# Split pieces of v kept in DRAM by the backward scan for the forward scan, and the head norm of o moved to ScalarE, in a hybrid Fourier and gated-linear-attention encoder

## The chip, the cores and the metric

One core of a Trainium2 chip runs the whole program. The metric is the device time of one execution in microseconds (us), lower is better. PE is TensorE, PEld its weight loads, DVE is VectorE, ACT is ScalarE, POOL is GpSimd, and SP is SyncE, whose in-order queue issues nearly all of the DMAs here.

## The reference

One encoder layer on x (1 x 2048 x 1024), all in float32, and a final RMSNorm. Cut to what matters here:

```
h    = rmsnorm(x) * (1 + scale) + shift
proj = h @ w_in                     # u, z, q, k, v, r and two gate logits
y_f  = fourier_mix(u) * silu(z)
o    = gla(q, k, v, forward) + flip(gla(flip q, flip k, flip v, backward, strict))
o    = o * rsqrt(mean(o*o, per head) + EPS)        # 4 heads of 256 values
y_g  = o * norm_g * silu(r)
x    = x + gate * (concat(y_f, y_g) @ w_out)
out  = rmsnorm(x)
```

`gla` is a chunked linear attention: per chunk, masked scores times v, plus the decayed query times a running state, and the state is updated with the decayed key (transposed) times v.

## The kernel before

The sequence is cut into 16 pieces of 128 rows, numbered `sc`, and into 8 blocks `blk` of two pieces. The 4 heads are worked in two pairs, `hp` = 0 and 1. Every product that needs float32 accuracy is made of three passes over split operands: `hi` is the operand rounded to the matmul type by an ACT copy, `lo` is the rest, by a DVE subtraction (helper `split`, L47 to L49), and the passes are hi.hi, hi.lo and lo.hi. So v has the pieces `vh` and `vl` of 128 x 512, made in `load_v` (L577) from `v`, which comes from the DRAM tensor `v_d` (`vd_`).

In order of the program: projections of the second half of the rows; the backward scan over blocks 7 to 4 (`scan_back`, L589) mixed with further projections (`block_col`, L272, whose weights `raw` are loaded, split into tiles `B` and stored to `bcol_d` for the other half); the Fourier branch and the projections of the first half; the backward scan over blocks 3 to 0, mixed first with projections and then with the splitting of the output weights (`wot` to `wo_hi`, `wo_lo`, L1044 to L1049) and six pieces of the Fourier part of the output projection (`out_fourier`); then the forward scan over the 16 pieces. In the forward scan piece `sc` runs through `core_fwd` (L750: loads, scores `sc`, `sf`, its split `sh` and `sl`, the products `on`, and `update`, which transposes the key to `ktr`, splits it to `kth` and `ktl`, makes `upd` on PE and `state` on DVE), then `tail_fwd` (L795: squares `jk` on ACT, `rstd` on POOL, the head norm of `o`, transposes `otr` on PE, product with `sr` on DVE), then `split_y` (`ghi`, `glo`), and one piece later `out_fwd` (L862: 96 or 192 matmuls `po`, L842, on `ghi`, `glo` and, for pieces not done ahead, `fhi`, `flo`; then `gated_add`, L847 and L848, and the last norm). `prework` (L484) prepares queries and keys of a block with `Exp` and `Ln` on ACT and many steps on DVE.

The order on each engine isn't the order of the code: the build lists all instructions by a scheduler of its own, with its own idea of how long each takes, and hands out buffers as it goes. So an edit at one place can move instructions far from it. On the chip each engine, and the SP queue, then works its list strictly in order; an instruction that waits holds up all that stand behind it.

Buffers that matter: `v`, `vh`, `vl`, `o` and (in the full form) `S` have two each; `v`'s two are also used for `y`, the Fourier part of `load_yf`. A buffer of `vh` is free when the last `upd` matmul that reads it is done.

Of the kernel before, what the change touches and what calls it, by code (L numbers as in the profile page):

```python
# [12 lines left out]
F32 = mybir.dt.float32  # L13
F32R = mybir.dt.float32r
BF16 = mybir.dt.bfloat16
U8 = mybir.dt.uint8
AF = mybir.ActivationFunctionType
ALU = mybir.AluOpType
# [3 lines left out]
P = 128  # L22
# [13 lines left out]
def hybrid_kernel(ctx, tc, i, out):  # L36
    nc = tc.nc
    V, S, G, T = nc.vector, nc.scalar, nc.gpsimd, nc.tensor
    KO = tc.keep_in_program_order

    def load(dst, src):
        nc.sync.dma_start(dst, src)

    def store(dst, src):
        nc.sync.dma_start(dst, src)

    def split(hi, lo, src, eng=None):  # L47
        S.activation(hi, src, AF.Copy)  # L48
        (eng or V).tensor_tensor(lo, src, hi.bitcast(F32), ALU.subtract)  # L49
# [9 lines left out]
    dram = ctx.enter_context(tc.tile_pool(name="dram", bufs=1, space=DRAM))  # L59
# [11 lines left out]
    od_ = dram.tile([16, 2, P, 512], F32, name="ob_d")  # L71
    sst_ = dram.tile([2, P, 512], F32, name="st_d")
    xd_ = dram.tile([16, P, D], F32, name="xf_d")
    us_ = dram.tile([P, NG, 16, 2, P], F32, name="us_d")
    bc_ = dram.tile([12, 7, P, 1024], F32, name="bcol_d")
    bt_ = dram.tile([4, 14, P, BW], F32, name="btok_d")
# [468 lines left out]
    def scores(d, pre, s):  # L545
        qi, ki, Q, K, _ = pre
        ps = pg.tile([P, 2, 192], F32, tag="sc", name="sc")
        kof, qof = (0, 128) if d == 0 else (64, 0)
        for h in range(2):
            g = 2 * h + s  # L550
            c0 = h * 256 + s * P
            T.matmul(ps[:, h, 0:128], ki[:, c0:c0 + P], qi[:, c0:c0 + P], start=True, stop=True)  # L552
            T.matmul(ps[:, h, 128:192], K[:, g, kof:kof + P], Q[:, g, qof:qof + 64], start=True, stop=True)  # L553
        return ps

    def update(d, pre, s, v, state, first):
        K, dec = pre[3], pre[4]
        kof = 64 if d == 0 else 0
        tp = pg.tile([P, 512], F32, tag="tr", name="ktr")
        kth = gp_.tile([P, 2, P], F32R, tag="kth", name="kth", bufs=1)  # L560
        ktl = gp_.tile([P, 2, P], F32R, tag="ktl", name="ktl", bufs=1)
        for h in range(2):
            T.transpose(tp[:, h * P:(h + 1) * P], K[:, 2 * h + s, kof:kof + P], ident[:])
        split(kth[:], ktl[:], tp[:, 0:256].rearrange("p (h t) -> p h t", h=2))
        up_ = pg.tile([P, 2, 256], F32, tag="big", name="upd", bufs=n_v)
        for h in range(2):
            hs = slice(h * 256, (h + 1) * 256)
            mm3(up_[:, h, :], [(kth[:, h, :], ktl[:, h, :], v[0][:, hs], v[1][:, hs])])
        for h in range(2):
            if first:  # L570
                V.tensor_copy(state[:, h, :], up_[:, h, :])
            else:
                g = 2 * h + s
                V.scalar_tensor_tensor(state[:, h, :], state[:, h, :], dec[:, g:g + 1], up_[:, h, :],  # L574
                                       ALU.mult, ALU.add)

    def load_v(sc, hp):  # L577
        v = gp_.tile([P, 512], F32, tag="v", name="v", bufs=n_v)
        load(v[:], vd_[sc, :, hp * 512:(hp + 1) * 512])
        vh = gp_.tile([P, 512], F32R, tag="vh", name="vh")  # L580
        vl = gp_.tile([P, 512], F32R, tag="vl", name="vl")
        S.activation(vh[:], v[:], AF.Copy)  # L582
        V.tensor_tensor(vl[:], v[:], vh[:].bitcast(F32), ALU.subtract)
        return vh, vl

    def states():
        return [gp_.tile([P, 2, 256], F32, tag=f"state{h}", name=f"state{h}", bufs=1) for h in range(2)]

    def scan_back(blk, hp, gt, st_b):  # L589
        pre = prework(1, blk, hp, gt)  # L590
        for s in (1, 0):
            sc = 2 * blk + s
            v = load_v(sc, hp)
            ps = scores(1, pre, s)
            sb = gp_.tile([P, 2, P], F32, tag="S", name="sb", bufs=n_v)
            S.activation(sb[:], ps[:, :, 0:128], AF.Copy)
            V.tensor_copy(sb[64:128, :, 0:64], ps[64:128, :, 128:192])
            store(sd_[sc, hp], sb[:].rearrange("p h t -> p (h t)"))
            if sc != 15:
                ob = pg.tile([P, 2, 256], F32, tag="big", name="ob", bufs=n_v)  # L600
                for h in range(2):
                    T.matmul(ob[:, h, :], pre[2][:, 2 * h + s, 64:192], st_b[hp][:, h, :],
                             start=True, stop=True)
                obs = gp_.tile([P, 512], F32, tag="o", name="obs")
                S.activation(obs[:], ob[:].rearrange("p h t -> p (h t)"), AF.Copy)
                store(od_[sc, hp], obs[:])
            if sc != 0:
                update(1, pre, s, v, st_b[hp], sc == 15)
# [141 lines left out]
    def core_fwd(sc, pre, st_f):  # L750
        s = sc % 2
        os_ = []
        for hp in range(2):
            v = load_v(sc, hp)
            sb = gp_.tile([P, 2, P], F32, tag="S", name="sf", bufs=n_v)
            load(sb[:].rearrange("p h t -> p (h t)"), sd_[sc, hp])
            ps = scores(0, pre[hp], s)
            V.copy_predicated(sb[:], mask[:].rearrange("p (h t) -> p h t", h=2), ps[:, :, 0:128])
            V.tensor_copy(sb[0:64, :, 64:128], ps[0:64, :, 128:192])
            sh = gp_.tile([P, 2, P], F32R, tag="sh", name="sh", bufs=1)  # L760
            sl = gp_.tile([P, 2, P], F32R, tag="sl", name="sl", bufs=1)
            split(sh[:], sl[:], sb[:])
            on = pg.tile([P, 2, 256], F32, tag="big", name="on", bufs=2)
            for h in range(2):
                hs = slice(h * 256, (h + 1) * 256)
                for k, (a_, b_) in enumerate(((sh, v[0]), (sh, v[1]), (sl, v[0]))):
                    T.matmul(on[:, h, :], a_[:, h, :], b_[:, hs], start=(k == 0), stop=(sc == 0 and k == 2))  # L767
                if sc != 0:
                    T.matmul(on[:, h, :], pre[hp][2][:, 2 * h + s, 0:128], st_f[hp][:, h, :],  # L769
                             start=False, stop=True)  # L770
            o = gp_.tile([P, 512], F32, tag="o", name="o")
            onf = on[:].rearrange("p h t -> p (h t)")
            if sc != 15:
                load(o[:], od_[sc, hp])
                V.tensor_tensor(o[:], o[:], onf, ALU.add)  # L775
                update(0, pre[hp], s, v, st_f[hp], sc == 0)
            else:
                V.tensor_copy(o[:], onf)
            os_.append(o)
        return os_  # L780

    def rstd(ss, n, width):
        r = op.tile([P, 4], F32, tag="rstd", name="rstd", bufs=4)
        G.tensor_scalar(r[:, 0:n], ss, 1.0 / width, EPS, ALU.mult, ALU.add)  # L784
        G.tensor_tensor(r[:, 0:n], r[:, 0:n], mhalf[:, 0:n], ALU.pow)  # L785
        return r
# [8 lines left out]
    def tail_fwd(sc, os_, sr):  # L795
        for hp in range(2):
            o = os_[hp]
            ss = op.tile([P, 2], F32, tag="ss", name="ss", bufs=4)
            for h in range(2):
                jk = op.tile([P, 512], BF16, tag="jk", name="jk", bufs=1)  # L800
                S.activation(jk[:, 0:256], o[:, h * 256:(h + 1) * 256], AF.Square, accum_out=ss[:, h:h + 1])  # L801
            r = rstd(ss[:], 2, 256)
            for h in range(2):
                V.tensor_scalar(o[:, h * 256:(h + 1) * 256], o[:, h * 256:(h + 1) * 256], r[:, h:h + 1], None,  # L804
                                ALU.mult)
            tp = pg.tile([P, 4, P], F32, tag="tr", name="otr")
            for c in range(4):
                T.transpose(tp[:, c, :], o[:, c * P:(c + 1) * P], ident[:])  # L808
            y = sr[:, 4 * hp:4 * hp + 4, :]
            V.tensor_tensor(y, tp[:], y, ALU.mult)  # L810
        return sr
# [280 lines left out]
    gt = gates(0)  # L1092
    pre = [prework(0, 0, hp, gt) for hp in range(2)]
    os_ = core_fwd(0, pre, st_f)
    for sc in fo:
        out_fourier(sc)
# [86 lines left out]
```

## Time and profile before

| | |
|---|---|
| median of 3 runs | 1669.92 us (1668.64 to 1671.33) |
| the profiled execution: its own time | 1670.82 us |
| the profiled execution: its span | 1669.0 us |
| granted TensorE clock, mean | 0.978 |
| PE busy | 1570.0 us, 94% |
| DVE busy | 1176.3 us, 70% |
| ACT busy | 695.7 us, 42% |
| DMA moved | 399.90 MB, mean 240 GB/s |

The span is the time from the first to the last instruction; what lies around it is 1.8 us. A share of busy time is a mean over stages, so the stages are read one by one: the backward scan with projections from about 205 to 440 us, its second part from about 1030 to 1200 us, the forward scan from about 1200 to 1640 us, and an end of 29 us. An engine that stands idle costs nothing unless PE waits for it, so the waits of PE come first.

### The profile page before, as it was taken

The page shows a single profiled execution, that of the slowest core. Times are in us where ns is not written, and L with a number is a line of the kernel's source. Part 1 is how long each engine was busy: PE and PEld are TensorE (multiplying, and loading weights), DVE is VectorE, ACT ScalarE, POOL GpSimd, SP SyncE. Part 2 cuts the span into 40 slices and gives each one's busy share as a digit, 9 for nine tenths or more (in the row PEclk, how much of TensorE's full clock was granted, in tenths as well). Part 3 has the DMA queues.
Part 4 walks back from the last instruction along what each step waited for, and adds up shares of the span by engine and source line. Part 5 has one row for each costly group of instructions (what it writes and reads, how often), then busy time and mean ns, then how long its engine had stood idle before and what let it go on. Part 6 is the DMA issues. An engine that isn't in the chain of part 4 may idle for free. (4 is left out here: it accounts for less than half of the span.)

```text
span 1669.0 us, 25145 instructions
## 1 busy us (share of the span) xinstructions
PE 1570.0 (94%) x9012; PEld 1352.1 (81%) x9012; DVE 1176.3 (70%) x2424; ACT 695.7 (42%) x1295; POOL 60.4 (4%) x118
## 2 busy tenths in 40 slices
PE   7899999999988999989989999979989999999997
PEld 5599878888888979889988888767868778878876
DVE  3976687898588265868775646678876776777673
ACT  4724244544244011323232317676644554555442
POOL 0000000000000000000000000000011111101110
PEclk9999999999999999999999999979999999999999
DMA  9599788888885799797888598777653434434422
GB/s 347 201 358 391 264 310 324 321 300 289 306 325 214 255 338 326 235 315 255 272 267 269 172 325 286 236 239 246 226 160 128 123 130 133 147 96 145 143 89 76
DMA packets 220044, 399.90 MB, mean 240 GB/s; under 512 B 19472, under 2 KB 121744, under 8 KB 216336
## 3 DMA queue, kind: packets, MB, share of 16 engines
q1 hardware_dynamic: 219776, 398.04, 69.3%
q8 instruction: 71, 1.16, 0.3%
q14 instruction: 53, 0.43, 0.1%
q10 hardware_dynamic: 144, 0.26, 0.0%
HBM read 237.60 MB, written 160.63 MB: 239 GB/s over the span
## 5 line engine op out<-in xcount | busy, mean ns | idle before, releaser
L272 PE MATMUL pj<-A_hi,B 128*128 128x512 f32 x1344 | 435.9, 399 | 6.7 <-ACT B L48 2.8
L315 PE MATMUL pj<-B,A_hi 128*128 128x264 f32 (+1 forms) x1792 | 336.7, 288 | 21.1 <-ACT p L322 5.8
L315 PEld LDWEIGHTS pj<-B,A_hi 128*128 128x128 f32 x1792 | 282.9, 192 | 26.9 <-ACT p L322 6.5
L272 PEld LDWEIGHTS pj<-A_hi,B 128*128 128x128 f32 x1344 | 251.8, 189 | 64.8 <-ACT B L48 3.7
L272 PE MATMUL pj<-A_lo,B 128*128 128x512 f32 x672 | 268.2, 399 | 0.0
L315 PE MATMUL pj<-B,A_lo 128*128 128x264 f32 (+1 forms) x896 | 255.3, 287 | 2.3 <-DVE A_lo L49 2.3
L315 PEld LDWEIGHTS pj<-B,A_lo 128*128 128x128 f32 x896 | 172.4, 193 | 2.5 <-DVE A_lo L49 2.5
L272 PEld LDWEIGHTS pj<-A_lo,B 128*128 128x128 f32 x672 | 126.8, 189 | 27.4 <-issue 0.2
L842 PE MATMUL po<-wo_hi,fhi 128*128 128x512 f32 x256 | 108.5, 424 | 11.0 <-ACT fhi L48 7.3
L842 PE MATMUL po<-wo_hi,ghi 128*128 128x512 f32 x256 | 103.9, 406 | 2.0 <-ACT ghi L48 2.0
L842 PE MATMUL po<-wo_lo,fhi 128*128 128x512 f32 x256 | 105.1, 411 | 0.0
L842 PE MATMUL po<-wo_lo,ghi 128*128 128x512 f32 x256 | 102.7, 401 | 0.0
L842 PE MATMUL po<-wo_hi,flo 128*128 128x512 f32 x256 | 92.5, 418 | 3.4 <-DVE flo L49 3.1
L842 PE MATMUL po<-wo_hi,glo 128*128 128x512 f32 x256 | 87.8, 407 | 4.3 <-DVE glo L49 4.3
L276 DVE TENSOR_TENSOR u<-u,pj 128x512 f32<-128x512 f32 x96 | 65.6, 683 | 23.2 <-PE pj L272 22.9
L48 ACT ACTIVATE B<-raw 128x512 fp32r<-128x512 f32 x72 | 43.6, 627 | 90.8 <-DMA raw<-in_w_in 41.0
L574 DVE SCALAR_TENSOR_TENSOR state<-state,sm,upd 128x256 f32<-128x256 f32 x112 | 48.8, 475 | 35.4 <-PE upd L56 35.0
L582 ACT ACTIVATE vh<-v 128x512 fp32r<-128x512 f32 x64 | 39.9, 625 | 79.8 <-PE upd L56 69.8
L842 PEld LDWEIGHTS po<-wo_hi,fhi 128*128 128x128 f32 x256 | 50.6, 197 | 24.4 <-ACT fhi L48 9.5
L320 DVE TENSOR_TENSOR u<-u,pj 128x264 f32<-128x264 f32 (+1 forms) x96 | 48.6, 511 | 30.9 <-PE pj L315 30.8
L56 PE MATMUL mapA<-PQ,wm 128*128 128x256 f32 x480 | 66.0, 287 | 1.4 <-ACT gp L48 1.3
L784 POOL TENSOR_SCALAR rstd<-ss 128x2 f32<-128x2 f32 (+1 forms) x48 | 15.8, 330 | 1365.6 <-ACT jk L801 1364.2
(221 smaller groups left out, 3081.6 us busy)
## 6 DMA issues: line engine op xcount, KB each, us to landing
bcol_d<-B SPq DMA_DIRECT2D x84, 512.0 KB, 4.1
B<-bcol_d SPq DMA_DIRECT2D x84, 512.0 KB, 5.1
v<-v_d SPq DMA_DIRECT2D x64, 256.0 KB, 3.3
btok_d<-B SPq DMA_DIRECT2D x28, 528.0 KB, 8.3
B<-btok_d SPq DMA_DIRECT2D x28, 528.0 KB, 6.9
btok_d<-B SPq DMA_DIRECT2D x28, 512.0 KB, 4.1
B<-btok_d SPq DMA_DIRECT2D x28, 512.0 KB, 5.9
raw<-in_w_in SPq DMA_DIRECT2D x12, 1024.0 KB, 7.8
```

Source lines behind the costliest of these rows:

```text
L48: S.activation(hi, src, AF.Copy)
L56: T.matmul(ps, a, b, start=(k == 0), stop=(k == n - 1))
L272: T.matmul(ps[:], B[k][0][:, bq, p, :], A[k][aq][:, p, :], start=(p == 0 and q == 0), stop=(p == 3 and q == 2))
L276: V.tensor_tensor(o, a, ps[:], ALU.add)
L315: T.matmul(ps[:, j, :], A[k][aq][:, p, t * P:(t + 1) * P], B[k][p // 2][:, bq, p % 2, :], start=(p == 0 and q == 0), stop=(p == 3 and q == 2))
L320: V.tensor_tensor(o[:, cut], a[:, cut], ps, ALU.add)
L574: V.scalar_tensor_tensor(state[:, h, :], state[:, h, :], dec[:, g:g + 1], up_[:, h, :], ALU.mult, ALU.add)
L582: S.activation(vh[:], v[:], AF.Copy)
L784: G.tensor_scalar(r[:, 0:n], ss, 1.0 / width, EPS, ALU.mult, ALU.add)
L842: T.matmul(ps[n][:], a, wo[j0 + j][q][:, cs], start=(first and a is yh and q == 0), stop=(last and a is yl))
```

## The change

Two edits. `load_v`, now used by the backward scan alone, stores both pieces of v to a new DRAM tensor `vs_d`; the forward scan calls the new `load_split_v`, which loads the two pieces and does no splitting. And in `tail_fwd` the two multiplications of o by `rstd`, one for each head, are ACT copies with a scale instead of DVE multiplications.

```diff
+    vs_ = dram.tile([16, 2, 2, P, 512], F32, name="vs_d")
...
         S.activation(vh[:], v[:], AF.Copy)
         V.tensor_tensor(vl[:], v[:], vh[:].bitcast(F32), ALU.subtract)
+        for n, x in enumerate((vh, vl)):
+            store(vs_[sc, hp, n], x[:].bitcast(F32))
         return vh, vl
+
+    def load_split_v(sc, hp):
+        v = [gp_.tile([P, 512], F32R, tag=n, name=n) for n in ("vh", "vl")]
+        for n, x in enumerate(v):
+            load(x[:].bitcast(F32), vs_[sc, hp, n])
+        return v
...
-            v = load_v(sc, hp)
+            v = load_split_v(sc, hp)
...
             for h in range(2):
-                V.tensor_scalar(o[:, h * 256:(h + 1) * 256], o[:, h * 256:(h + 1) * 256], r[:, h:h + 1], None,
-                                ALU.mult)
+                S.activation(o[:, h * 256:(h + 1) * 256], o[:, h * 256:(h + 1) * 256], AF.Copy, scale=r[:, h:h + 1])
```

Over the whole program DVE has 32 subtractions `vl` and 64 multiplications of o fewer, ACT has 32 copies `vh` fewer and 64 scaled copies of o more, and SP issues 64 stores to `vs_d` more and, in place of 32 loads of `v`, 64 loads of `vh` and `vl`. PE has the same 8500 matmuls. From the first backward scan on, the scheduler lists all engines but POOL in another order. Line numbers of the changed program are higher by 1 above `load_v` and by 8 or 9 below it.

ACT, forward scan, the second of the pieces that take `Silu` of `sr` there (L792 before, L801 now), before:

```order
L792 ACT_TABLE_LOAD
L792 ACTIVATE sr<-sr 128x1024
L482 ACT_TABLE_LOAD
L582 ACTIVATE vh<-v 128x512
L48 ACTIVATE kth<-ktr 128x256
L512 ACTIVATE sm<-sm 128x8
L801 ACTIVATE jk,ss<-o 128x256 x2
```

and now:

```order
L801 ACT_TABLE_LOAD
L801 ACTIVATE sr<-sr 128x1024
L483 ACT_TABLE_LOAD
L513 ACTIVATE sm<-sm 128x8
L48 ACTIVATE kth<-ktr 128x256
L515 ACTIVATE pa<-pb 128x512
L810 ACTIVATE jk,ss<-o 128x256
L520 ACTIVATE pb<-pb 128x512
L810 ACTIVATE jk,ss<-o 128x256
L496 ACTIVATE pa<-lg 128x512
L499 ACTIVATE pa<-pa 128x512
L813 ACTIVATE o<-o,rstd 128x256 x2
```

The copy `vh` that stood ahead of `kth` is gone, and the two scaled copies of o stand three instructions behind the second square.

SP, forward scan, the loads for one piece ahead of a store of the output, before:

```order
L42 DMA v<-v_d 128x512
L42 DMA sf<-sb_d 128x256
L42 DMA v<-v_d 128x512
L42 DMA qi<-q_d 128x512
L42 DMA ki<-k_d 128x512
L893 DMA out_dram<-xr 128x1024
```

and now:

```order
L42 DMA vl<-vs_d 128x512
L42 DMA vh<-vs_d 128x512
L42 DMA sf<-sb_d 128x256
L42 DMA gf<-g_d 128x256
L42 DMA vl<-vs_d 128x512
L42 DMA vh<-vs_d 128x512
L42 DMA o<-ob_d 128x512
L42 DMA qi<-q_d 128x512
L42 DMA ki<-k_d 128x512
L901 DMA out_dram<-xr 128x1024
```

Each load of v has become two loads, which stand next to each other.

SP, first backward scan, from the stores of one weight block to the load of the next `raw`, before:

```order
L45 DMA bcol_d<-B 128x1024 x4
L42 DMA v<-v_d 128x512
L45 DMA sb_d<-sb 128x256
L45 DMA bcol_d<-B 128x1024 x2
L45 DMA ob_d<-obs 128x512
L42 DMA raw<-in_w_in 128x2048
```

and now:

```order
L45 DMA vs_d<-vh 128x512
L45 DMA bcol_d<-B 128x1024 x3
L45 DMA vs_d<-vl 128x512
L45 DMA sb_d<-sb 128x256
L42 DMA v<-v_d 128x512
L45 DMA ob_d<-obs 128x512
L45 DMA bcol_d<-B 128x1024 x2
L42 DMA raw<-in_w_in 128x2048
```

Two stores to `vs_d` have come in ahead of the load of `raw`, the second of which waits for the DVE subtraction `vl`.

## Rows read from the trace of the kernel before

**Rows 1.** The page's busy times by engine, whole span.

```profile
PE 1570.0 (94%) x9012; PEld 1352.1 (81%) x9012; DVE 1176.3 (70%) x2424; ACT 695.7 (42%) x1295; POOL 60.4 (4%) x118
```

**Rows 2.** Table of stretches: us; busy of PE, PEld, DVE, ACT, POOL; clock; DMA share; GB/s.

```profile
205.00:440.00 235.00, 231.24 (x1128) 191.96 (x1127) 190.87 (x361) 97.76 (x193) 0.00 (x0) 0.99 0.84 302
1030.00:1200.00 170.00, 155.56 (x753) 128.08 (x751) 127.64 (x240) 114.52 (x177) 0.00 (x0) 0.94 0.74 248
1200.00:1640.00 440.00, 415.12 (x2150) 346.89 (x2151) 310.23 (x655) 213.90 (x453) 54.14 (x104) 0.98 0.41 130
```

**Rows 3.** Waits of PE, 1200 to 1640 us: us in total, times, longest us.

```profile
PE po L842 <- ACT fhi L48: 4.6, 4, 1.4
PE po L842 <- DVE glo L49: 4.3, 2, 2.5
PE sc L552 <- DVE sf L759: 3.6, 2, 1.9
PE po L842 <- DVE xr L848: 3.6, 3, 1.5
PE po L842 <- DVE flo L49: 2.3, 3, 1.7
PE upd L56 <- DVE ktl L49: 2.2, 1, 2.2
PE po L842 <- ACT ghi L48: 2.0, 2, 1.8
PE sc L552 <- DVE ki L521: 1.1, 1, 1.1
PE upd L56 <- ACT kth L48: 0.9, 1, 0.9
PE otr L808 <- DVE sr L810: 0.8, 2, 0.5
PE on L767 <- DVE sl L49: 0.8, 1, 0.8
```

**Rows 4.** DVE in order of time around 1362 us: start us, us, engine, line, instruction.

```profile
1361.02 0.67 DVE L583 TENSOR_TENSOR vl<-v,vh 128x512 fp32r<-128x512 f32 x1
...
1363.20 0.69 DVE L49 TENSOR_TENSOR glo<-sr,ghi 128x512 fp32r<-128x512 f32 x1
```

**Rows 5.** PE in order of time at the same place; in brackets idle before, releaser.

```profile
1363.94 0.51 PE L842 MATMUL po<-wo_hi,glo 128*128 128x512 f32 x1 [2.52 <-DVE glo L49]
```

**Rows 6.** ACT groups, 1200 to 1669 us: count | busy us, mean ns | idle before, releasers.

```profile
L801 ACT ACTIVATE jk<-o 128x256 bf16<-128x256 f32 x64 | 26.4, 412 | 17.3 <-DVE o L775 15.3 <-DVE o L778 0.7 <-DVE sl L49 0.3
...
L582 ACT ACTIVATE vh<-v 128x512 fp32r<-128x512 f32 x30 | 18.8, 626 | 55.6 <-PE upd L56 50.9 <-PE on L767 4.7
```

**Rows 7.** DVE groups, 1200 to 1669 us.

```profile
L583 DVE TENSOR_TENSOR vl<-v,vh 128x512 fp32r<-128x512 f32 x30 | 20.5, 683 | 2.8 <-ACT vh L582 2.7
L804 DVE TENSOR_SCALAR o<-o,rstd 128x256 f32<-128x256 f32 x64 | 19.8, 350 | 19.1 <-POOL rstd L785 19.0
```

**Rows 8.** An ACT copy of 128x256 with a per-row scale, Fourier branch, 600 to 1000 us.

```profile
L700 ACT ACTIVATE tw<-us,vecs 128x256 f32<-128x256 f32 x28 | 14.2, 508 | 51.8 <-DMA us<-us_d 42.9 <-DVE gp L49 6.2 <-DVE PQ L49 2.5
```

**Rows 9.** Stretches of 20 us, columns as in rows 2.

```profile
100.00:120.00 20.00, 18.57 (x148) 17.94 (x147) 11.97 (x24) 3.86 (x8) 0.00 (x0) 1.00 1.02 405
...
720.00:740.00 20.00, 15.98 (x79) 13.82 (x78) 11.72 (x28) 1.80 (x4) 0.00 (x0) 0.85 1.06 345
...
980.00:1000.00 20.00, 20.00 (x87) 16.10 (x86) 9.58 (x17) 3.53 (x6) 0.00 (x0) 1.00 1.02 365
```

**Rows 10.** DMA issues, 1200 to 1640 us: KB each, median us to landing.

```profile
v<-v_d SPq DMA_DIRECT2D x29, 256.0 KB, 2.8
```

**Rows 11.** Waits of the SP queue, 1200 to 1640 us: us in total, times, longest us.

```profile
SPq L42 <- DVE vl L583: 20.4, 10, 3.7
```

**Rows 12.** PE in order of time at the change from projections to output projection.

```profile
1098.76 0.80 PE L552 MATMUL sc<-qi,ki 128*128 128x128 f32 x2 [5.06 <-DVE sb L597]
...
1106.26 0.58 PE L56 MATMUL upd<-vh,ktl 128*128 128x256 f32 x1 [1.26 <-DVE ktl L49]
```

## The prediction

> **What bounds the kernel now.** I read the page's busy times first, then the table of stretches, then PE's waits stage by stage, and only then the engines it waits for. PE is busy for 94% of the span, DVE for 70%, ACT for 42% [rows 1]. The change adds no matmul and removes none, so it can only win where PE stands still or runs at the lower clock. In the three stages that it touches PE stands still for 3.8 us (235 less 231.24), 14.4 us (170 less 155.56) and 24.9 us (440 less 415.12) [rows 2]. The forward scan is thus the place to look. PE's waits there add up to 26.2 us, 18.7 us on DVE in 15 waits and 7.5 us on ACT in 7 [rows 3]; none is on a DMA directly. The granted clock there is 0.98 of 2.4 GHz, so about (1 - 0.98) x 440 = 8.8 us more go to stretches at 1.2 GHz, if PE is what counts throughout. About 35 us is everything that could be won in this stage.
>
> **The DVE work that goes.** In the forward scan 30 of the 32 subtractions vl stand in the stretch, 20.5 us, and all 64 multiplications of o, 19.8 us [rows 7]. Together they are 40.3 us, 13% of DVE's 310.23 us [rows 2]. DVE is not the bound, so this isn't the gain. What it is worth is seen where PE waits: at 1363.94 us PE had waited 2.52 us for glo [rows 5], and in the row of DVE work that had piled up before that glo stands one vl, which holds the queue for 0.6 us or so [rows 4]. Taking it away shortens that wait by about a quarter. I find a removed instruction, worth 0.3 to 0.7 us, in the pile ahead of about every second DVE wait that I followed, some of them with more than one. So I take a third of the 18.7 us, 6.2 us. The bounds are 0 (the scheduler fills the room with other DVE work, which then stands in front) and 18.7 us.
>
> **The ACT work that goes and comes.** The copies vh go: 18.8 us of work, and with them 55.6 us in which ACT stood before a vh, 50.9 of it until an upd matmul freed the buffer [rows 6]. Whatever was listed behind vh stood too; the order shows a vh right ahead of a kth, and PE waited for kth once, 0.9 us [rows 3]. The scaled copies come: 64 at 508 ns, the price of the same shape with a per-row scale [rows 8], 32.5 us. ACT goes from 214 us [rows 2] to about 228 of 440 us, still half empty. The wait for rstd from POOL, 19.0 us before the DVE multiplications [rows 7], moves onto ACT's queue with them; behind the waiting copies stand sh, ghi, kth and the exponentials of the next block, and PE waits for these through DVE. In the new order at most a few instructions stand between the second square and the copies, so each of the 32 places can hold ACT for up to the time of two POOL steps. The freed queue and the new wait are of one size, 55.6 against 19.0 us of standing plus 14 us of work, and I take them as even: 0, with bounds of -7.5 us (all waits on ACT go) and +10 us (a third of a us lost at each of the 32 places).
>
> The forward chain of one piece is on, o, squares, rstd, norm, otr. The norm in it takes two steps of 508 instead of 350 ns, 0.3 us more; between on and otr the new order leaves at least 22 matmuls, where the old one left at least 19, and at 415.12 us for 2150 matmuls, 0.19 us each [rows 2], the 0.3 us is covered except at the closest few places. The Trainium skill, "ScalarE: Activation LUTs", Rules for kernel authors, says to do multiplications on VectorE, not on ScalarE; it speaks against this edit. By it the norm should stay, and the sum would lose its 32 x 0.3 = 10 us if the norm were always last; in this trace ACT is slower per instruction too, 508 against 350 ns, but it is the emptier engine, and the sum goes by that.
>
> **The clock.** Fewer and shorter waits mean fewer stretches at 1.2 GHz. In proportion, 6.2 of 26.2 us of the 8.8, some 2 us. Bounds 0 and 8.8. The forward scan gives 6.2 + 0 + 2 = 8 us.
>
> **The loads of the forward scan.** One load of v, 2.8 us to landing [rows 10], becomes two, on the same SP queue. The v buffers used to be filled well ahead, held up only by the subtraction that emptied them (20.4 us of SP's waits [rows 11]); now vh and vl are filled only when the last upd of the piece before last has read them, and all loads behind them in the queue (sf, o, qi, ki) stand meanwhile. From that upd to the on that needs the new pieces the order leaves at least 41 matmuls, 8 us at 0.19 us, against 2 x 2.8 = 5.6 us if the two don't overlap at all. DMA rises from 130 x 440 us = 57 MB by 30 x 0.26 = 8 MB, from 0.41 to 0.47 of its time [rows 2]. Cost 0; without that cover up to 5.6 us at a place. At the turn from backward to forward, pieces must be stored before they are loaded; the matmuls of out_fourier lie between, and I cost it at 0, at most 5.6 us.
>
> **The stores of the first backward scan.** 16 units store two pieces each, 8.4 MB, on top of 302 x 235 us = 71 MB, which takes the DMA share from 0.84 to about 0.94 [rows 2]. SP's queue holds a store until vl is done, and behind it stand the stores of B, the loads of v and the load of raw, on which the next block's first matmul hangs. Between 100 and 1000 us there are ten stretches of 20 us with a share of 1.00 or more; PE stood still in them for 8.4 us together, from 0 to 4.0 us each [rows 9], 0.84 us on average. Over 235 us that is 9.9 us, 6 us more than the 3.8 of today: the upper bound. The lower bound is 0, since the share stays under 1. I take +2 us.
>
> **The second backward scan.** 8.4 MB on 248 x 170 us = 42 MB, share 0.74 to 0.89 [rows 2]. The worst place is where projections end and the output projection begins: PE waited 5.06 us for a copy sb that stood on DVE behind four wo_lo [rows 12], and later 1.26 us for ktl. In the new order three wo_lo stand ahead of the first such sb, which is a gain of about one DVE step, but three scan steps' scores, not two, come before the output projection, and the stores of vl stand ahead of loads of y and wot in SP's queue. I take +1 us, bounds -3 (the 5.06 us wait shrinks by half) and +8 (it comes twice and the clock with it: the stage's clock of 0.94 costs (1 - 0.94) x 170 = 10 us already [rows 2]).
>
> **Sum.** -8 + 2 + 1 = -5 us on the profiled execution's 1670.8 us (span 1669.0 and 1.8 around it): 1665.8. That execution lies 0.9 us above the median of the runs, so the forecast is 1665 us.
>
> **Rivals.**
>
> One: the queues free up more than the DVE third. For it: nearly every wait of PE in the forward scan ends on a split by DVE or ACT that stood in a pile [rows 3], both piles shrink, and the order has moved too: places with fewer than ten matmuls from ktr to upd are one now, three before, and with at most twenty matmuls from sc to on one instead of five. Against it: glo, flo, xr and fhi aren't relieved by the order. Half of the 26.2 us and of the 8.8 us, 17 us, less 2 us in the backward scans, gives 1655 us.
>
> Two: the gain goes nowhere, because the norm's wait for POOL takes over on ACT what vl and vh cost. ACT then holds sh, ghi and kth back by up to 0.3 us at 32 places, some of it ahead of PE: the 6.2 us are eaten, and with the backward scans' 3 us less 2 us of clock the time is about 1670 us. For it: the 19.0 us of waiting for rstd [rows 7]. Against it: ACT's 55.6 us that vanish [rows 6].
>
> Three, slower: the backward scans fill the DMA. The stores push the share in 205 to 440 us over 1, raw and wot come late, and PE starves as in the ten stretches: +6 us there and +8 us at the change to the output projection, less the forward gain of 8: +6, about 1676 us. It decides from a share of 1.0 in that stage; 0.94 speaks against it, the 720 to 740 us stretch [rows 9], with PE idle 4.0 us and the clock at 0.85, for it.
>
> **How the numbers follow.** The forecast gets 0.50, rival one 0.13, rival two 0.17, rival three 0.20. A measurement tells about 0.2% from no change here, 3.3 us: faster is under 1666.6, slower over 1673.3. Of the forecast's 0.50 I put 0.43 under 1666.6 and 0.07 above. Faster is 0.43 + 0.13 = 0.56, same 0.07 + 0.17 = 0.24, slower 0.20. The range runs from 1653 (a little beyond rival one) to 1677 us (rival three); the forecast's own is 1659 to 1668.
>
> **What would show it.** PE's waits in the forward scan fall to about 20 us, those on glo, xr and ktl most; DVE's busy time in the stage falls by 40 us and ACT's rises by about 14; ACT's idle time before the scaled copies, until rstd, is near 19 us, and none is left before a vh there. PE's idle time in 205 to 440 us stays under 8 us and the DMA share near 0.94. I am wrong if PE waits there for raw or B by more than that, if PE's waits in the forward scan do not fall, or if on waits for a load of vh or vl.

## The result, and the profile after

The changed kernel takes 1652.05 us (median of 6 runs, 1648.71 to 1656.02), the kernel before 1669.82 us (6 runs, 1665.51 to 1671.33). The ratio is 0.9898, 95% interval 0.9882 to 0.9914: 17.8 us faster. The direction was as forecast, the size was not: 5 us were forecast, and the time lies 1 us under the low end of the range.

The first three fences are of the changed kernel's profile. Its page, busy times by engine:

```profile
PE 1559.2 (94%) x9012; PEld 1349.2 (82%) x9012; DVE 1142.0 (69%) x2328; ACT 699.6 (42%) x1324; POOL 53.8 (3%) x118
```

The page lists the same number of PE records, 9012, in 1559.2 us of busy time instead of 1570.0 [rows 1]. The matmuls are the same, so each took less time on average; the granted clock in the rows below goes with that. Now the table of stretches, columns as in rows 2, with the stage between them (440 to 1030 us), which the prediction did not look at:

```profile
205.00:440.00 235.00, 230.00 (x1123) 190.46 (x1122) 188.59 (x360) 96.25 (x195) 0.00 (x0) 0.99 0.93 337
440.00:1030.00 590.00, 555.03 (x3745) 511.72 (x3744) 394.72 (x891) 175.93 (x307) 0.00 (x0) 0.98 0.82 276
1030.00:1200.00 170.00, 154.63 (x737) 127.89 (x737) 128.06 (x241) 111.06 (x172) 0.00 (x0) 0.93 0.87 294
1200.00:1640.00 440.00, 432.13 (x2284) 365.68 (x2283) 289.48 (x582) 228.12 (x498) 49.37 (x109) 1.00 0.47 155
```

In the forward scan PE stands still for 7.9 of 440 us; before it was 24.9 [rows 2]. PE's waits there (us in total, times, longest us):

```profile
PE sc L553 <- DVE sf L768: 2.7, 1, 2.7
PE otr L816 <- ACT jk L880: 1.5, 1, 1.5
PE po L850 <- DVE xr L856: 1.0, 2, 0.8
PE sc L553 <- DVE ki L522: 0.9, 1, 0.9
PE on L776 <- DVE sl L49: 0.8, 1, 0.8
PE otr L816 <- DVE sr L818: 0.6, 1, 0.6
PE sc L554 <- DVE K L543: 0.4, 1, 0.4
```

They add up to 7.9 us, against 26.2 [rows 3]. In this kernel every wait for glo, flo, ghi, fhi, ktl and kth is gone, not a third of them.

Fixed stretches shift against each other when work ahead of them takes longer, so from here on I cut each trace at its first on matmul, the start of the forward scan. The row of that part, of the kernel before and then of the changed one:

```profile
1205.70:1669.00 463.30, 428.85 (x2210) 357.68 (x2208) 316.33 (x662) 215.72 (x460) 56.89 (x112) 0.97 0.39 125
```

```profile
1215.70:1651.20 435.50, 418.16 (x2215) 353.79 (x2213) 283.05 (x567) 223.45 (x492) 50.31 (x112) 0.99 0.46 150
```

The forward part gained 27.8 us: 17.1 of standing (34.5 to 17.3) and 10.7 of PE's busy time, with the granted clock at 0.99 instead of 0.97. But it began 10.0 us later (1215.7 against 1205.7), so what lies ahead of it lost that much. The forecast had -8 and +3. Both terms were too small, and they lean against each other.

### The profile page after: what moved, and what is told of

Its sections match the earlier page's. It is cut to its first block, busy times and chain, and to the rows that moved or that the text cites. A ratio compares the mean times of both kernels' runs of the same rounds, so it can differ in the third digit from the quotient of the medians.

```text
span 1651.2 us, 25169 instructions
## 1 busy us (share of the span) xinstructions
PE 1559.2 (94%) x9012; PEld 1349.2 (82%) x9012; DVE 1142.0 (69%) x2328; ACT 699.6 (42%) x1324; POOL 53.8 (3%) x118
## 4 chain that ended last, share of the span: by engine, by line
PE 41%; DMA 12%; DVE 10%; ACT 5%; issue 3%; SPq 1%; POOL 0%; DVEq 0%; POOLq 0%; ACTq 0%
PE po L850 18%; PE pj L273 7%; PE pj L316 6%; DMA us<-us_d 3%; DMA wot<-in_w_out 1%; PE mapA L56 1%; DMA us_d<-U 1%; PE on L778 1%; PE upd L56 1%; PE pq L56 1%; PE on L776 1%; DMA B<-btok_d 1%; DMA B<-bcol_d 1%; PE sc L553 1%; DVE A_lo L49 1%
## 5 line engine op out<-in xcount | busy, mean ns | idle before, releaser
L850 PE MATMUL po<-wo_hi,fhi 128*128 128x512 f32 x256 | 105.1, 412 | 4.8 <-ACT fhi L48 3.8
L48 ACT ACTIVATE B<-raw 128x512 fp32r<-128x512 f32 x72 | 42.8, 625 | 74.4 <-DMA raw<-in_w_in 26.2
L553 PE MATMUL sc<-qi,ki 128*128 128x128 f32 x256 | 55.2, 298 | 10.4 <-DVE sb L606 6.6
L56 PEld LDWEIGHTS mapA<-PQ,wm 128*128 128x128 f32 x480 | 61.8, 193 | 2.6 <-ACT PQ L48 1.2
## 6 DMA issues: line engine op xcount, KB each, us to landing
xs<-in_xT SPq DMA_DIRECT2D x16, 512.0 KB, 10.7
```

The source lines that it names most:

```text
L56: T.matmul(ps, a, b, start=(k == 0), stop=(k == n - 1))
L850: T.matmul(ps[n][:], a, wo[j0 + j][q][:, cs], start=(first and a is yh and q == 0), stop=(last and a is yl))
```

## The experiments

The theories. **Work (A):** each removed instruction gives back part of its own time, because it stands in a pile that PE waits for. **What v held up (B):** ACT stood for 55.6 us before vh, until an upd had freed the buffer [rows 6], and whatever was listed behind it stood too; v also shared its two buffers with y. **Listing (C):** the planner (the build's scheduler) lists the whole scan anew after any edit, and the gain is a lucky list. For the loss ahead of the scan: **traffic** of the stores, or again the **listing**.

Four kernels were run first; the forward parts are measured as above, each in one profiled execution. A result is the median time, then its ratio to runs of the kernel before made beside it (medians 1670.96 to 1674.13 us), with the 95% interval.

**Pieces alone** (e1): the changed kernel with the norm on DVE.

```
-  S.activation(o[...], o[...], AF.Copy, scale=r[:, h:h + 1])
+  V.tensor_scalar(o[...], o[...], r[:, h:h + 1], None, ALU.mult)
```

> Only the pieces of v are stored and loaded; the norm of o stays on DVE. The forward part, from the first on matmul to the end of the span, is 463.3 us before and 435.5 us in the changed kernel. Theory A (removed work, each edit by the DVE time it takes away, 20.5 and 19.8 us): half of the 27.8 us, forward part about 450 us, whole time about 1663 us with the 10 us that the changed kernel loses ahead of the forward scan. Theory B (what v held up: ACT standing 55.6 us before vh, and the two v buffers that y shares): nearly all of it, forward part 435 to 440 us, whole time about 1653 us. Theory C (the new listing, not the work): any value.

1663.82 us, 0.9955 (0.9933 to 0.9976); forward part 443.9 us, first on at 1220.7. The time is that of theory A; the forward part lies between the two.

**Norm alone** (e2): the kernel before with the norm on ACT; v is split in both scans, nothing is stored.

```
-  V.tensor_scalar(o[...], o[...], r[:, h:h + 1], None, ALU.mult)
+  S.activation(o[...], o[...], AF.Copy, scale=r[:, h:h + 1])
```

> Only the norm of o goes to ACT; v is split in both scans, nothing is stored. Theory A: forward part about 449 us, whole time about 1656 us. Theory B: forward part 460 to 466 us, whole time 1667 to 1673 us. Theory C: any value. All: DMA as before, 205 to 440 us as before.

1662.55 us, 0.9947 (0.9928 to 0.9966); forward part 452.8 us, first on at 1213.8. Both lie between the theories.

**Stores alone** (e3): the backward scan stores the pieces, the forward scan splits v again, the norm is on DVE.

> The backward scan stores the pieces, the forward scan doesn't use them and is as before. This prices the stores. Theories A and B: forward part 460 to 466 us, whole time 1670 to 1680 us, the stores cost 0 to 10 us, all of it ahead of the forward scan. Theory C: the forward part moves by more than 8 us though its work is the same.

1679.94 us, 1.0056 (1.0039 to 1.0073), slower than the kernel before: 9.0 us, where 3 were forecast. First on at 1219.9. The forward part takes 459.6 us, 3.7 under that of the kernel before.

**One store** (e4): the changed kernel, but only one unit's pieces are stored, and every load reads these.

```
-  for n, x in enumerate((vh, vl)):
+  for n, x in enumerate((vh, vl) if sc == 15 and hp == 0 else ()):
...
-  load(x[:].bitcast(F32), vs_[sc, hp, n])
+  load(x[:].bitcast(F32), vs_[15, 0, n])
```

> The changed kernel with the store of one unit alone; all forward loads read that one, so the result leaves out the other units' values. 62 of 64 stores are gone. If the stores' traffic costs the 10 us ahead of the forward scan (PE waiting 10.9 us for the copy p at 460 to 480 us): whole time about 1642 us, and that wait is 5 us or less. If it is the new listing: 1648 to 1656 us, the wait still there or another in its place. Forward part 435 us in both.

1655.19 us, 0.9911 (0.9885 to 0.9936). The wait for p fell to 5.1 us, as expected for traffic, and the time stayed where the listing was to put it. First on at 1205.6, so the loss ahead of the scan goes with the stores, by their traffic or by the list that they bring. But the forward part takes 447.9 us, 12 more than the changed kernel with the same work in another list: single runs of the edits prove less than they seem to.

The next four kernels went after the two causes.

**DVE back** (e5): one operation in place on each loaded vl, of the size of the subtraction that was removed.

```
+  V.scalar_tensor_tensor(vl, vl.bitcast(F32), 0.0, vl.bitcast(F32), ALU.mult, ALU.add)
```

> The changed kernel, and in the forward scan one DVE operation in place on each loaded vl (128x512, vl times 0 plus vl), so DVE again has 32 operations of the kind that the 32 subtractions were, ahead of each piece's use, while ACT stays free of vh. The pieces alone gave 16 us more than the stores cost (1663.82 against 1679.94 us). Theory A (the gain of the pieces is DVE's work in the piles ahead of its splits): most of it goes, 1660 to 1668 us, forward part 445 to 452 us instead of 435.5, and PE waits on flo, fhi, glo again. Theory B (the gain is that ACT stands no more behind vh, and DVE's work hides): 1652 to 1656 us, forward part 436 to 440 us.

1674.36 us, 1.0017 (1.0003 to 1.0031): the whole gain is gone, more than either theory expected. The forward part's row and the added group (busy us, mean ns, idle before it and releasers):

```profile
1217.70:1676.90 459.20, 428.73 (x2212) 360.47 (x2211) 299.40 (x596) 223.36 (x492) 58.51 (x112) 0.97 0.44 142
```

```profile
L594 DVE SCALAR_TENSOR_TENSOR vl<-vl 128x512 fp32r<-128x512 f32 x30 | 20.6, 685 | 5.7 <-DMA vl<-vs_d 5.2
```

20.6 us of DVE work cost 23.7 us against the changed kernel, though DVE is busy for only 299 of 459 us; the profiled execution was the slowest of ten, 4.3 us over their median. A queue that is a third idle can still be the one that PE waits for. PE's waits for DVE in the forward part are back at 16.4 us, but at other places than expected: on sf (5.9), sr (4.7) and ki (3.7), none on glo, flo or fhi.

**ACT back** (e7): one copy in place on each loaded vh.

```
+  S.activation(v[0][:], v[0][:].bitcast(F32), AF.Copy)
```

> The changed kernel, and in the forward scan one ACT copy in place on each loaded vh (128x512), so ACT has its 32 instructions again, each of which holds ACT's queue until the load has landed and through it until the buffer is free, while DVE stays free of vl. Theory A (DVE's work): nothing of the gain goes but what ACT's 19 us cost by themselves, 1652 to 1656 us, forward part 436 to 440 us. Theory B (ACT's standing before vh): most of the pieces' 16 us goes, 1662 to 1668 us, forward part 446 to 452 us, ACT idle before these copies some 50 us.

1666.86 us, 0.9969 (0.9957 to 0.9982); forward part 449.2 us, 13.7 more than the changed kernel. Its row among ACT's groups:

```profile
L593 ACT ACTIVATE vh<-vh 128x512 fp32r<-128x512 f32 x30 | 18.8, 626 | 16.1 <-DMA vh<-vs_d 13.6 <-PE sc L554 2.5
```

ACT stood for 16.1 us here, not the 55.6 of the kernel before, so this gives ACT its work back, but only part of its standing. Neither theory holds alone: a DVE instruction at the head of each piece costs PE about its own time, an ACT one somewhat less. Both kernels list the forward scan in their own way, and each new instruction also waits for its load, so neither number is the price of the subtraction or of the copy in the kernel before.

**One buffer for y** (e10): half of what v and y used to share is held by another tile.

```
+  hold = gp_.tile([P, 512], F32, tag="v", name="hold", bufs=n_v)
+  V.memset(hold[:], 0.0)
   ...the forward scan...
+  V.tensor_copy(hold[:, 0:1], hold[:, 1:2])
```

> The changed kernel, and one of the two buffers that v and y share is held by a tile of its own through the forward scan, so y has one buffer there and not two. In the kernel before, v took both of them in turn with y. If part of the gain is that y (the copy of the output projection's result on its way to the store) has both buffers to itself, PE waits longer on po, or ACT and DVE on y, and the time rises by 5 us or more, to 1657 or above. If not: 1651 to 1654 us, no difference.

1655.42 us, 0.9907 (0.9888 to 0.9927), between the two expectations. The forward part settles it: 435.8 us against 435.5, with ACT and DVE in the same order in both. y's second buffer is worth nothing; the 3 us lie ahead of the scan, where nine kernels with this list, all but for single instructions, begin their first on between 1214.0 and 1220.7 us, so they are not the buffer's.

This run leaves the other half of the sharing open: v is gone from these buffers in it too. ACT's copies fhi of y, in the kernel before and in the changed one (busy us, mean ns, idle before them and releasers), show what v did there:

```profile
L48 ACT ACTIVATE fhi<-y 128x512 fp32r<-128x512 f32 x20 | 12.6, 629 | 22.0 <-DMA y<-yf_d 21.9
```

```profile
L48 ACT ACTIVATE fhi<-y 128x512 fp32r<-128x512 f32 x22 | 13.8, 629 | 18.0 <-PE po L850 17.8
```

In the kernel before ACT stood for 21.9 us until y had landed; now y is there in time. It is so in every trace: in the seven kernels that load v in the forward scan ACT stood 14.2 to 27.6 us for y, and PE 2.5 to 7.5 us for fhi. In the twelve that load the pieces ACT stood for y 1.5 us at most, and PE waited for no fhi and no flo, not even in e5 and e7, which put DVE's or ACT's work back. So these waits came with v and not with the work of its split alone. Right ahead of two of the four on fhi in the kernel before ACT had stood for y itself, 2.98 and 1.57 us, so a late load of y beside v is the likely cause; ACT's standing before vh (theory B) is the other. No run separates the two.

**p first** (e8): the a_affine of the second block may be listed only behind the last copy of t1 of the first.

```
+  with tc.issue_after(t1_copies[-1].ins):
       for p in range(4):
           x_scale(xs[p], rb)
           a_affine(p, xs[p])
```

The reason for it is in the two traces around 460 us, ACT in order of time (start us, us, line and instruction). The kernel before, then the changed one:

```profile
460.96 2.38 ACT L180 ACTIVATE xs<-xs,vecs 128x1024 f32<-128x1024 f32 x2 [0.57 <-DVE xs L171]
463.25 1.06 ACT L322 ACTIVATE p<-pj 128x512 f32<-128x512 f32 x2
464.20 1.23 ACT L180 ACTIVATE xs<-xs,vecs 128x1024 f32<-128x1024 f32 x1
```

```profile
463.48 2.38 ACT L181 ACTIVATE xs<-xs,vecs 128x1024 f32<-128x1024 f32 x2 [1.29 <-DVE xs L172]
465.76 0.61 ACT L48 ACTIVATE B<-traw 128x512 fp32r<-128x512 f32 x1
466.28 2.36 ACT L181 ACTIVATE xs<-xs,vecs 128x1024 f32<-128x1024 f32 x2
468.54 0.61 ACT L48 ACTIVATE B<-traw 128x512 fp32r<-128x512 f32 x1
469.06 1.23 ACT L181 ACTIVATE xs<-xs,vecs 128x1024 f32<-128x1024 f32 x1
470.19 0.61 ACT L48 ACTIVATE B<-t 128x512 fp32r<-128x512 f32 x1
470.71 1.23 ACT L181 ACTIVATE xs<-xs,vecs 128x1024 f32<-128x1024 f32 x1
471.85 1.05 ACT L323 ACTIVATE p<-pj 128x512 f32<-128x512 f32 x2
```

The copies p empty the PSUM banks (the memory that PE writes its products to) that PE's next pj needs. In the changed kernel six of the long L181 and three splits stand ahead of them instead of two L180. PE's row behind them (in brackets its idle time) and the 20 us around it, columns as in rows 2, both of the changed kernel, and then that stretch of the kernel before:

```profile
472.47 0.80 PE L316 MATMUL pj<-B,A_hi 128*128 128x256 f32 x2 [10.92 <-ACT p L323]
```

```profile
460.00:480.00 20.00, 9.08 (x66) 8.89 (x65) 16.00 (x20) 13.61 (x17) 0.00 (x0) 0.74 0.69 270
```

```profile
460.00:480.00 20.00, 16.12 (x123) 16.13 (x124) 19.73 (x27) 14.40 (x18) 0.00 (x0) 0.91 0.75 297
```

The DMA isn't full there, 0.69; PE stands behind ACT's list. The wait is 10.9 us in every kernel that stores all pieces and keeps this order, 4.8 or 5.1 in those that don't store them all.

> The changed kernel with one order fixed: the four x_scale and a_affine of do_u(1, A, 0) may be listed only behind that block's last copy of t1, so that the copies of p out of pj stand on ACT ahead of the seven a_affine that stand ahead of them in the changed kernel, as in the kernel before. If PE's 10.9 us wait on ACT p at 460 to 472 us (4.8 in the kernel before, 5.1 with one store) comes from this listing: the wait falls to 5 us or less, the 20 us stretch has its clock back, and the time falls by 4 to 10 us, to 1642 to 1648 us. If it comes from the stores' traffic on the DMA: the wait stays at about 10 us and the time at 1650 to 1654 us. If a better listing there moves what follows, a gain at 460 us is given back in 500 to 1200 us.

1657.38 us, 0.9916 (0.9900 to 0.9933). The wait fell to 5.7 us, projections ended 4.8 us earlier (1093.3 against 1098.1), and the first on came at 1210.8 instead of 1215.7. The forward part then took 444.2 us, 8.7 more, and ate it. The third of the expected cases, then, but with the loss in the forward scan and not in 500 to 1200 us, unless that loss is scatter.

So the scatter of the lists had to be measured. Two edits that change no instruction, only the order in which the code names them, make the planner list the forward scan otherwise and leave everything ahead of it as it was:

```
on:   -  for h in range(2):          +  for h in (1, 0):
otr:  -  for c in range(4):          +  for c in (3, 2, 1, 0):
```

> The changed kernel with the two heads of on written in the other order in the forward scan: the same instructions, but the planner lists the forward scan otherwise from its first part on, and everything ahead of it as before. Two other listings of the changed kernel's forward scan (of the runs with one store and with p first) took 447.9 and 444.2 us where the changed kernel's own takes 435.5, the kernel before 463.3. If the gain is the removed work, all listings of the changed kernel lie well under all of the kernel before: here 435 to 448 us forward, total 1651 to 1664. If much of the gain is this one listing (a lucky one), 450 us or more, total over 1666.

> The changed kernel with the four transposes of otr written in reverse: the same instructions, another listing of the forward scan alone. Expected as in the run with on's heads reversed: 435 to 448 us forward if the gain is work, 450 or more if it is the listing.

The changed kernel: 1658.65 us, 0.9916 (0.9887 to 0.9946), with on's heads reversed and 1657.40 us, 0.9919 (0.9889 to 0.9948), with otr's transposes reversed.

> The kernel before with the two heads of on in the other order, its listing changed in the forward scan alone. If the changed kernel's gain is the removed work, this stays near the kernel before: 457 to 469 us forward, total 1664 to 1676. If the kernel before had an unlucky listing, 450 us or less forward and 1657 or less in total.

> The kernel before with the four transposes of otr written in reverse, its listing changed in the forward scan alone. Expected as in the run of the kernel before with on's heads reversed: 457 to 469 us forward if the gain is work, 450 us or less if the listing of before was unlucky.

The kernel before: 1671.03 us, 0.9993 (0.9973 to 1.0013), and 1670.33 us, 0.9992 (0.9975 to 1.0008). No list of the kernel before comes near any of the changed one, 460.3 to 463.3 us forward against at most 447.9, though the otr edit moved little there (24 of 661 DVE records stand elsewhere).

> Norm alone on ACT, with the two heads of on in the other order: another listing of the forward scan alone. The first listing took 452.8 us forward. If the norm's move is work that PE feels, about half of the whole, all listings lie between the kernel before (459.6 to 463.3) and the changed one (435.5 to 447.9): 447 to 456 us. If the norm alone is worth nothing and the first listing was lucky: 458 us or more.

> Norm alone on ACT, with the transposes of otr in reverse, a third listing. Expected as in the run with on's heads reversed: 447 to 456 us forward if the norm is worth about half, 458 or more if it is worth nothing alone.

Norm alone: 1668.43 us, 0.9974 (0.9956 to 0.9992), and 1666.57 us, 0.9962 (0.9940 to 0.9983). Their forward parts, 459.0 and 454.2 us, fall one into "worth nothing" and one into "worth about half".

> Pieces alone (stored and loaded, the norm on DVE), with the transposes of otr in reverse, another listing of the forward scan alone. The first listing took 443.9 us forward. If the pieces are worth 15 us or more in the forward scan whatever the listing: 440 to 449 us. If the first listing was lucky: 452 us or more, and the pieces are worth 10 us or less, no more than the stores cost.

Pieces alone: 1668.57 us, 0.9974 (0.9962 to 0.9987), with 449.4 us forward, a touch over the expected 440 to 449.

> The changed kernel with the a_affine held behind the last copy of t1 (the run with p first) and the two heads of on in the other order. The run with p first was 4.8 us ahead of the changed kernel where the projections end, and lost 8.7 us of it in the forward scan, where its listing takes 444.2 us. If that loss is scatter between listings, this one draws again from 435 to 448 us: total 1645 to 1660 us, and ahead of the forward scan some 5 us less than the changed kernel in any case. If the p order itself costs the forward scan: 444 us or more again.

> As the run with p first and on's heads reversed, with the transposes of otr in reverse instead: 435 to 448 us forward if the loss was scatter between listings, total 1645 to 1660 us; 444 us or more if the p order costs the forward scan.

p first with two more lists: 1648.06 us, 0.9864 (0.9840 to 0.9888), and 1659.48 us, 0.9933 (0.9908 to 0.9958). The three lists of p first take 444.2, 434.4 and 445.4 us forward, so its order doesn't have to cost the forward scan. But two of the three are over 444, their mean is 441.3 against 437.6 of the three lists of the changed kernel, and the times have means of 1655.0 and 1656.0 us: a gain of p first in the whole time is not shown. The one with on's heads reversed is the fastest kernel of this study; it lies 4 us under the changed kernel by the medians, with intervals that still touch. Its forward part, and its waits there:

```profile
1212.00:1646.40 434.40, 418.43 (x2214) 353.65 (x2212) 282.65 (x567) 223.88 (x493) 51.50 (x112) 0.99 0.46 150
```

```profile
PE sc L554 <- DVE sf L769: 2.2, 3, 1.4
PE otr L817 <- ACT jk L881: 1.5, 1, 1.5
PE sc L554 <- DVE ki L523: 0.9, 1, 0.9
```

All lists together, forward part in us, from the row of each trace from its first on to its end (standing is length less PE's busy time; PE's waits are counted as in rows 3, over the same part):

| forward work | lengths by list | mean | PE standing, mean | PE busy, mean | PE's waits for DVE, mean | for ACT, mean |
|---|---|---|---|---|---|---|
| as before (before, on, otr, e3) | 463.3, 461.4, 460.3, 459.6 | 461.2 | 32.3 | 428.8 | 16.3 | 6.1 |
| norm on ACT (e2, on, otr) | 452.8, 459.0, 454.2 | 455.3 | 27.7 | 427.6 | 9.5 | 8.6 |
| pieces loaded (e1, otr) | 443.9, 449.4 | 446.7 | 22.9 | 423.8 | 11.8 | 1.5 |
| both (after, on, otr, e4, e8 and its two) | 435.5, 437.3, 440.1, 447.9, 444.2, 434.4, 445.4 | 440.7 | 20.4 | 420.3 | 8.2 | 2.8 |

By the means the norm is worth 5.8 us, the pieces 14.5 and both 20.5, about their sum. The norm's lists nearly touch those of before (459.0 against 459.6), but all three of its times are lower too, 0.9947 to 0.9974 with no interval that reaches 1. Lists of one kind differ by 4 to 13.5 us. Not all of that is the list, since one program's times scatter as well (the ten of e1 from 1656.16 to 1670.07 us); but the two last kernels with p first, 1645.89 to 1651.53 and 1658.70 to 1660.76 us, differ in the list alone and don't overlap. The changed kernel's own list is 5.2 us better than the mean of its kind and that of the kernel before 2.1 worse, so of its 27.8 us I estimate some 20 as work and some 7 as the list.

Ahead of the scan the same can be done with the time of the first on. Without stores (before, its two lists, the norm's three): 1205.7 to 1213.8, mean 1209.9. With all stores (nine traces, after, e1, e3, e5, e7, e10, the on and otr lists of the changed kernel and the otr list of the pieces): 1214.0 to 1220.7, mean 1217.6. With all stores and p first: 1210.8, 1212.0, 1211.5, mean 1211.4. The stores cost 7.7 us ahead of the scan, of which 6.2 come back when the copies p stand where they used to (an edit that lists other work anew too).

## Why the prediction was wrong in size

**The bound and the place: right.** PE's standing in the forward scan was the thing to win, and it was won there. What failed is the forward sum of 6.2 + 0 + 2 = 8 us: all three terms were too small. By the means of the table they are 8.1 (DVE), 3.3 (ACT) and 8.5 us (clock), 20 together.

**The DVE third: mis-sized.** I took 6.2 of the 18.7 us of waits for DVE, arguing that a pile of several instructions gets shorter by one of them. In the changed kernel's list the waits for DVE fell from 18.7 to 6.4 us, two thirds; by the means of the lists from 16.3 to 8.2, half, and PE stood 12 us less. As I read it, the picture of one pile was too small: a wait ends at a margin. Where a split was 0.5 us late behind a pile and the pile loses 0.6, the wait is gone and not shortened by a quarter. Twelve of the 22 waits in [rows 3] stand in groups whose longest wait is 1.5 us or less. Seven of the 22, on fhi and flo, went with v and likely with the late load of y, a path that the prediction did not have. e5 points the same way from the other side: the same DVE work put back costs 23.7 us against the changed kernel's list, or 18.5 against the mean of its kind, if at other places.

**ACT at 0: mis-sized.** I set the freed queue against the wait for rstd as even. Both sides are in the table: PE's waits for ACT rose by 2.5 us with the norm alone (6.1 to 8.6), fell by 4.6 with the pieces alone (to 1.5) and by 3.3 with both. The wait for POOL came as expected, 14.2 us (19 forecast), in 64 scaled copies at 501 ns (508 forecast). ACT's groups of the changed kernel:

```profile
L813 ACT ACTIVATE o<-o,rstd 128x256 f32<-128x256 f32 x64 | 29.0, 501 | 14.2 <-POOL rstd L794 14.1
L810 ACT ACTIVATE jk<-o 128x256 bf16<-128x256 f32 x64 | 26.5, 414 | 47.9 <-DVE o L784 44.2 <-DVE o L787 2.9
```

But standing isn't alike, as I read it: what ACT stood for before vh, the end of an upd, held back splits that PE needed, and what it stands for now, rstd and o, holds back work that PE needs later. The changed kernel has 47.9 us of idle ACT before the squares, and PE does not feel it. In its list the waits of PE for ACT fell from 7.5 us to one of 1.5.

**The Trainium skill's rule** ("ScalarE: Activation LUTs", Rules for kernel authors: multiplications go on VectorE). The trace agrees that the instruction itself is dearer, 501 against 350 ns. As a rule for this kernel following it would have given up 5.8 us by the means above: ACT had the room, and DVE's queue was the one that PE waited for more (16.3 against 6.1 us).

**The clock: mis-sized.** I gave back 2 of 8.8 us in proportion to the waits. PE's busy time for the same matmuls fell by 10.7 us, by 8.5 us in the means. With every us of standing 0.6 to 0.7 us of slower matmuls went too, but with the norm alone only 1.2 us with 4.6. Proportion was the wrong step: with the waits halved it would have given 4.4 of the 8.8. The 8.8 was itself a little low, since its stretch left out the end: from the first on, (1 - 0.97) x 463 is 14 us before and (1 - 0.99) x 435.5 is 4 after.

**The loads at 0: right.** SP's queue stands much longer for the end of an upd, in the changed kernel's row for 1200 to 1640 us (us in total, times, longest), against 20.4 us for vl [rows 11]:

```profile
SPq L42 <- PE upd L56: 123.3, 26, 8.8
```

and no wait of PE on a vh or vl is in the list. The queue had the time.

**The stores: +2 right, +1 too small, and the largest loss in no term.** In 205 to 440 us PE stood for 5.0 us (3.8 before) at a DMA share of 0.93, as forecast; in 1030 to 1200 for 15.4 (14.4 before). But fixed stretches hide work that comes late, so I compare starts of the same work, as means of the six traces without stores and the nine with all of them. PE's first matmul of the projections behind the scan starts at 447.2 and 449.3 us: 2.1 lost. Its wait for p at 460 us is 4.8 and 10.9: 6.1 more, through ACT's list. The projections end at 1094.2 and 1098.9, so some 3.5 of the loss come back on the way, and from that end to the first on it takes 115.7 and 118.7: 3.0 lost again. So +2 was about 2.1 and +1, behind the projections, about 3.0, and the 6.1 stood in no term: I had looked for the cost where the stores are, and in the order of before and after only at the places that I meant to cost. The hoped-for gain at the first sb didn't come, 5.3 us after 5.06, and that wait was misread: in it DVE itself stood for ACT, and then two wo_lo, not four, ran ahead of the sb. The first of them, in the kernel before:

```profile
1095.09 1.22 DVE L1045 TENSOR_TENSOR wo_lo<-wot,wo_hi 128x1024 fp32r<-128x1024 f32 x1 [3.30 <-ACT wo_hi L1044]
```

Rival three, that the stores fill the DMA over the whole stage, did not happen, though four of its stretches of 20 us reached a share of 1.00 to 1.03.

**The rivals.** The first, that the queues free up more than the DVE third, 1655 us, comes nearest to what happened, and its half of 26.2 and 8.8 us, 17, is near the 20.5 of the means. That its time is within 3 us is partly luck: the forward part gained 27.8 us and what lies ahead lost 10.0, where it had 17 and 2. I gave it 0.13, because I read that glo, flo, xr and fhi would not be relieved by the order; the three splits among them were, to nothing. The second, that the norm's wait takes over on ACT, is not borne out by the norm's kernels: PE waits 2.5 us more for ACT in them, but 6.8 less for DVE, and all three times are lower.

**What I said would show it.** PE's waits at about 20 us: 7.9. DVE 40 us less: 33.3 in the forward part (316.33 to 283.05), because the records of neighbours overlap (below). ACT 14 us more: 7.7. The waits on glo, xr and ktl fell most, as said, from 10.1 to 1.0 us, and with them those on fhi, which the list of signs did not have.

**What stays open.** How the pieces' 14.5 us divide between the subtraction, the copy, ACT's standing before vh and the load of y: e5 and e7 put 18.5 and 8.5 us over the mean of their kind, each with one list and with a wait for its load that the kernel before had not, and that is more than the whole. That the DVE part is larger than ACT's is likely from this, not shown. Why the planner moves the p copies when stores are added was not followed further.

## What to carry to other kernels

Where PE waits at many short places for a queue, taking work out of that queue can end waits that a share of the pile would only shorten: 40.3 us of DVE work removed were worth some 20 us, 12 of standing and 8.5 of matmuls at a higher clock, though DVE was busy for only 70%. The price differs by edit: 19.8 us of multiplications moved to ACT gave 5.8. For each wait, ask whether a pile or a late load stands behind it. Compare the order of instructions over the whole program, not only where the edit is: adding a store in one stage moved two copies behind nine other instructions in the next, which made one wait 6.1 us longer, more than was lost in either stage that has the stores. And where a planner lists the work anew after each edit, measure two or three lists of the same work before giving an edit a price: here they differed by up to 13.5 us, about as much as the larger edit is worth.

## What the runs showed of the hardware

DVE's records overlap. In the changed kernel, in order of time (start us, us):

```profile
1363.23 0.66 DVE L818 TENSOR_TENSOR sr<-otr,sr 128x512 f32<-128x512 f32 x1
1363.82 0.67 DVE L49 TENSOR_TENSOR glo<-sr,ghi 128x512 fp32r<-128x512 f32 x1
1364.41 0.27 DVE L768 COPY sf<-sc 64x128 f32<-64x128 f32 x1
```

Each 128x512 operation is listed with 0.66 or 0.67 us, and the next begins 0.59 us after it. A sum of such durations overstates what the queue is busy: 40.3 us of removed work [rows 7] took 33.3 us off DVE's busy time.
